# Summing two norms' squares over the partitions on GpSimd instead of TensorE

## The chip, the cores and the metric

The kernel runs on one core of one Trainium2 chip. The metric is the device time of one execution in microseconds; the median of a few runs stands for a kernel. A profiled execution gives, besides its own time, a trace of every instruction on every engine: TensorE (PE, with its weight loads as PEld), VectorE (DVE), ScalarE (ACT), GpSimd (POOL) and SyncE (SP), the last one only issuing transfers.

## The reference, cut to what matters

One layer of a streaming encoder is computed for a prompt of 256 frames and for 64 new frames of a running stream; the kernel treats them together as T = 320 columns. The model width D is 2048.

```python
def rmsnorm(x, g):
    x32 = x.astype(jnp.float32)
    y = x32 * lax.rsqrt(jnp.mean(x32 * x32, axis=-1, keepdims=True) + EPS)
    return (y * g.astype(jnp.float32)).astype(x.dtype)
...
    xn = rmsnorm(x, norm_mix[l])
    proj = xn @ w_in[l]
    q, k, v, u, vs, g = jnp.split(proj, [...], axis=-1)
    a = stick_breaking_prompt(q, k, v)          # or _sample, with the cache
    u = jax.nn.gelu(u)
    vs = rmsnorm(jax.nn.gelu(vs), sgu_norm[l])
    bb = spatial_gate(u, vs, w_spatial[l], b_spatial[l])
    gates = jax.nn.sigmoid(g + b_gate[l])
    merged = g_a * (a @ w_branch_a[l]) + g_b * (bb @ w_branch_b[l])
    h = x + merged @ w_out[l]
    hn = rmsnorm(h, norm_ffn[l])
    gu = hn @ w_gate_up[l]
    h = h + (jax.nn.silu(gu[..., :D_FF]) * gu[..., D_FF:]) @ w_down[l]
    return h, k, v, vs
```

After the layer a final RMSNorm follows. So there are four norms: of x (the first), of gelu(vs) over 1024 channels (the second), of h over 2048 (the third), and the final one.

## The kernel before, in words

Features lie on the 128 partitions, the 320 frames on the free axis. A norm needs, for each frame, the sum of squares over all features: first over the 128-feature tiles (elementwise adds into one 128x320 tile), then over the 128 partitions.

**Blocks.** All large products go through `block` (line 90): 128 output features, the sum over 16 (or 8, or 12) tiles of the input. Each weight tile is loaded by SP (line 80), 8 tiles of 128x128 at a time, into `raw`; ScalarE rounds it into `wh` (line 69) and VectorE writes the remainder `wl` (line 70). `product` (line 83) then issues three TensorE products for each tile: wh with the high part of the input (line 86), wh with the low part (line 87), wl with the high part (line 88). Eight tiles, so 24 products, are a half block here. `wh` and `wl` have four buffers each, `raw` three, and three more in the first part of the kernel. Block results go to three PSUM buffers `acc`, side results to `aux`.

**Ticks.** After each half block `tick()` (line 61) counts one up and issues what was put down for that tick with `at(...)`. This is how the side work is woven into the blocks by hand: attention (lines 293 to 381) at given ticks, and the second norm and the spatial gate as follows. `base` is the tick at which the last block of vs has been issued; at `base + 1` comes `sgu_norm` (line 444), at `base + 3 + 4p` `sgu_turn(p)` (scale vs by the norm and by its gain, store the new rows, transpose by DMA through SP), at `base + 5 + 4p` `sgu_join(p)` (VectorE puts the transposed halves together as `rows`), at `base + 6 + 4p` `sgu_mix(p)` (TensorE multiplies `rows` with the spatial weights, lines 464 and 465). The blocks of u run meanwhile. A scheduler turns the program into one queue for each engine and may move instructions of ScalarE and VectorE ahead of others in it.

**Norms.** `Squares.add` (line 152) squares a tile on ScalarE (lines 154, 157) and adds it to the total on GpSimd (line 158). `rms` (line 136) sums the total over the partitions: a product of a 128x128 tile of ones with the total, into the PSUM buffer `aux1` (line 138). That puts the sum on every partition. Then VectorE forms the mean plus EPS (line 140), ScalarE the square root (line 143), and `newton` (line 130) the reciprocal and a correction step on VectorE (lines 131 to 134). The first norm's sum is needed in the very first blocks (line 217, `rx`), the second by `sgu_turn` (line 450, `rv`), the third (line 533, `rh`) one tick into the first block of the FFN. The third norm is applied not before the FFN's products but after them, in `finish` (lines 542 and 545). The final norm has code of its own at the end and doesn't use `rms`.

**GpSimd** otherwise issues transfers: cache rows (lines 248, 251), k, v and sv stores (lines 400, 452), the residual x (line 526). It also sets the masks at the start. The kernel warms TensorE with products of ones at its start (line 167) and keeps it busy in the tail with some more (line 633).

Of the kernel before, what the change touches and what calls it, by code (L numbers as in the profile page):

```python
# [7 lines left out]

# [3 lines left out]
AF = mybir.ActivationFunctionType  # L12
ALU = mybir.AluOpType

P = 128
TP = 256
TS = 64
T = TP + TS
D = 2048
# [7 lines left out]
EPS = 1e-6  # L27
# [6 lines left out]
def stream_step(ctx: ExitStack, tc: tile.TileContext, xT, w_in, w_a, w_b, w_out, w_gu, w_down,  # L34
                gains, ws_t, bs, ck_t, cv, y_t, k_t, v_t, sv_t):
    nc = tc.nc
    pool = lambda name, bufs=1, **kw: ctx.enter_context(tc.tile_pool(name=name, bufs=bufs, **kw))
# [13 lines left out]
    def aux1():  # L51
        return psum.tile([P, 512], F32, tag="aux1", bufs=1, name="aux1")
# [13 lines left out]
    def halved(raw, n):  # L66
        wh = wsplit.tile([P, HALF * P], F32R, tag="wh", name="wh")
        wl = wsplit.tile([P, HALF * P], F32R, tag="wl", name="wl")
        nc.scalar.copy(out=wh[:, : n * P], in_=raw[:, : n * P])  # L69
        nc.vector.tensor_tensor(out=wl[:, : n * P], in0=raw[:, : n * P],  # L70
                                in1=wh[:, : n * P].bitcast(F32), op=ALU.subtract)
        return wh, wl
# [10 lines left out]
    def product(ps, w, j, x, first, last):  # L83
        wh, wl = w
        a, b = wh[:, j * P : (j + 1) * P], wl[:, j * P : (j + 1) * P]
        nc.tensor.matmul(ps[:, :T], a, x[0], start=first, stop=False)  # L86
        nc.tensor.matmul(ps[:, :T], a, x[1], start=False, stop=False)  # L87
        nc.tensor.matmul(ps[:, :T], b, x[0], start=False, stop=last)  # L88

    def block(src, act):  # L90
        ps = acc()
        nk = len(act)
        for k0 in range(0, nk, HALF):
            n = min(HALF, nk - k0)
            w = weights(src[:, k0 * P : (k0 + n) * P], n)
            for j in range(n):
                product(ps, w, j, act[k0 + j], k0 + j == 0, k0 + j == nk - 1)
            tick()
        return ps[:, :T]
# [4 lines left out]
    def pair(name, shape=(2, T), dt=F32):  # L104
        return big.tile([P, *shape], dt, tag="D", bufs=24, name=name)

    def gained(src, gain):
        hi, lo = slot("A"), slot("A")
        nc.scalar.activation(out=hi, in_=src, func=AF.Copy, scale=gain)  # L109
        nc.vector.scalar_tensor_tensor(out=lo, in0=src, scalar=gain, in1=hi.bitcast(F32),  # L110
                                       op0=ALU.mult, op1=ALU.subtract)
        return hi, lo

    def t320(tag, bufs=2, dt=F32):
        return tmp.tile([P, T], dt, tag=tag, bufs=bufs, name=tag)

    ones = const.tile([P, P], F32, name="ones")
# [5 lines left out]
    eps_t = const.tile([P, 1], F32, name="eps_t")  # L123
# [6 lines left out]
    def newton(r, ms, e):  # L130
        nc.vector.reciprocal(out=r, in_=r)
        nc.vector.scalar_tensor_tensor(out=e, in0=ms, scalar=-0.5, in1=r, op0=ALU.mult, op1=ALU.mult)
        nc.vector.tensor_tensor(out=e, in0=e, in1=r, op=ALU.mult)
        nc.vector.scalar_tensor_tensor(out=r, in0=e, scalar=1.5, in1=r, op0=ALU.add, op1=ALU.mult)

    def rms(name, total, width):
        ps = aux1()
        nc.tensor.matmul(ps[:, :T], ones, total, start=True, stop=True)
        ms = t320("ev")
        nc.vector.tensor_scalar(out=ms, in0=ps[:, :T], scalar1=1.0 / width, scalar2=EPS,  # L140
                                op0=ALU.mult, op1=ALU.add)
        r = const.tile([P, T], F32, tag="rms", bufs=2, name=name)
        nc.scalar.activation(out=r, in_=ps[:, :T], func=AF.Sqrt, bias=eps_t, scale=1.0 / width)
        newton(r, ms, t320("bb"))
        return r

# [14 lines left out]
    got = {}  # L161
    attn: dict[int, dict] = {0: {}}
    first = [[acc(), aux(), aux()], [acc(), aux(), aux()]]
    totx = const.tile([P, T], F32, tag="total", bufs=2, name="totx")
# [8 lines left out]
    def load_x(i, a=0, b=2):  # L173
        if i not in xp:
            xp[i] = pair("x")
        nc.sync.dma_start(out=xp[i][:, a:b, :], in_=xT[:, 2 * i + a : 2 * i + b, :])

    def load_w(b0, nb, c, n):
        raw = rpool.tile([P, HALF * P], F32, tag="raw1", bufs=9, name="raw1")
        nc.sync.dma_start(out=raw[:, : nb * n * P].rearrange("p (b k) -> p b k", b=nb),  # L180
                          in_=w_in[b0 : b0 + nb, :, c * P : (c + n) * P].rearrange("b p k -> p b k"))
        return raw

    def square(i):
        if i == 0:
            squares.append(pair("sqx"))
            nc.scalar.activation(out=squares[0], in_=xp[0], func=AF.Square)
        else:
            t = pair("xx")
            nc.scalar.activation(out=t, in_=xp[i], func=AF.Square)  # L190
            nc.vector.tensor_tensor(out=squares[0], in0=squares[0], in1=t, op=ALU.add)
# [6 lines left out]
    with tc.manual_schedule(engines={mybir.EngineType.SP}):  # L198
        load_x(0, 0, 1)
        for i, (b0, nb, c, n) in enumerate(tiles):  # L200
            raw = load_w(b0, nb, c, n)
            for more in behind.get(i, ()):
                load_x(*more)
            if i == len(tiles) - 1:
                for name, src in (("ck", ck_t[:, 0 : 2 * PAST]), ("cv", cv[:, :, 0 : 2 * P])):
                    attn[0][name] = t = pair(name, (2, PAST))
                    nc.sync.dma_start(out=t if name == "cv" else t.rearrange("p h t -> p (h t)"), in_=src)
            if i == 0:
                xs.append(gained(xp[0][:, 0, :], g_mix[:, 0:1]))
                lead = halved(raw, n)  # L210
                continue
            w = halved(raw, nb * n)
            for m in range(len(xs), c + n):
                xs.append(gained(xp[m // 2][:, m % 2, :], g_mix[:, m : m + 1]))
            if c + n == KD and b0 == 0:
                nc.vector.tensor_tensor(out=totx, in0=squares[0][:, 0, :], in1=squares[0][:, 1, :], op=ALU.add)
                got["rx"] = rms("rx", totx, D)
            if i == 1:
                for j in range(n):
                    for h, a in enumerate((lead, w)):  # L220
                        product(first[h][0], a, j, xs[j], j == 0, False)
                continue
            for b in range(nb):
                for j in range(n):
                    product(first[(b0 + b) % H][(b0 + b) // H], w, n * b + j, xs[c + j], c + j == 0, c + j == KD - 1)
            for m in done_squares.get(i, ()):
                square(m)
# [205 lines left out]
    for g in range(H):  # L433
        ps = block(w_in[4 * H + g], xs)
# [9 lines left out]
    def sgu_norm():  # L444
        got["rv"] = rms("rv", sq.total, H * P)
# [41 lines left out]
    for g in range(H):  # L487
        ps = block(w_in[3 * H + g], xs)
# [6 lines left out]
    for m in range(KD):  # L495
        gate = []
        for i in range(2):
            ps = block(w_in[5 * H + i * KD + m], xs)
# [9 lines left out]
        ps = block(w_a[m], aT)  # L508
        t = t320("mg", 1)
        nc.vector.tensor_tensor(out=t, in0=ps, in1=gate[0], op=ALU.mult)  # L510
        ps = block(w_b[m], bT)
# [10 lines left out]
    for m in range(KD):  # L522
# [4 lines left out]
        ps = block(w_out[m], merged)  # L527
# [3 lines left out]
        sq.add(hs[m])  # L531
    mctx.close()
    at(state["tick"] + 1, lambda: got.update(rh=rms("rh", sq.total, D)))

    sqf = Squares("sq_f")
# [68 lines left out]
    for s0, n in SLICES:  # L604
# [7 lines left out]
        for m in range(KD - LATE if final else KD):  # L612
            ps = block(w_down[m][:, s0 * P : (s0 + n) * P], halves)
# [24 lines left out]
    def root(ps, w):  # L638
        r, e = (const.tile([P, w], F32, name=f"{x}{w}") for x in "re")
        nc.scalar.activation(out=r, in_=ps[:, 0:w], func=AF.Abs_reciprocal_sqrt, scale=1.0 / D)  # L640
        nc.vector.scalar_tensor_tensor(out=e, in0=ps[:, 0:w], scalar=-0.5 / D, in1=r, op0=ALU.mult, op1=ALU.mult)
        nc.vector.tensor_tensor(out=e, in0=e, in1=r, op=ALU.mult)
        nc.vector.scalar_tensor_tensor(out=r, in0=e, scalar=1.5, in1=r, op0=ALU.add, op1=ALU.mult)
        return r
# [15 lines left out]
    with tc.manual_schedule(engines={mybir.EngineType.PE, mybir.EngineType.DVE, mybir.EngineType.Activation,  # L660
# [10 lines left out]
        r = root(sums, 2)  # L671
# [26 lines left out]
        r = root(sums, 1)  # L698
# [60 lines left out]
```

## Time and profile before

| | |
|---|---|
| median of 3 runs | 1705.58 us (1705.47 to 1706.55) |
| the profiled execution | 1705.79 us |
| its span, first to last instruction | 1704.0 us |
| granted TensorE clock, mean | 0.999 |
| TensorE busy | 1694.5 us, 11560 instructions |
| VectorE busy | 879.7 us, 1110 instructions |
| ScalarE busy | 673.8 us, 838 instructions |
| GpSimd busy | 54.9 us, 89 instructions |

How to read the lines that follow: in a timeline, a line gives the start and the length in microseconds, the engine, the line of the program, the operation, output tile<-input tiles, the shape, and how many instructions are merged in it; in brackets stands how long the engine had been idle before and what ended that. In a list of groups, the numbers behind the bar are the busy time in us, the mean length of one in ns, and the idle time before them. In a list for one line of the program, three lengths in ns are the shortest, the median and the longest. A line of the windows gives, for a stretch of time, the busy time of each engine with its number of instructions, the granted TensorE clock, the share of the DMA engines and GB/s.

### The profile page before, as it was taken

The numbers are of one execution on the slowest core, as the hardware profiler recorded it, in microseconds if no ns is written. First come the engines' busy times: TensorE is split into PE (matmuls) and PEld (weight loads), VectorE is DVE, ScalarE is ACT, GpSimd is POOL, SyncE is SP. The second block draws the span as 40 slices with busy tenths as digits, with TensorE's granted clock in tenths as the row PEclk, the third lists the DMA queues.
The fourth block names the chain that finished last, engine by engine and source line by source line (L and its number), as shares of the span: only waits on it lengthen the run. The fifth ranks groups of instructions, "written<-read, shape, count | busy, mean of one in ns | idle before, by whom it ended". The sixth has DMA issues, their size and how long they took to land.

```text
span 1704.0 us, 27430 instructions
## 1 busy us (share of the span) xinstructions
PE 1694.5 (99%) x11560; PEld 1690.2 (99%) x11560; DVE 879.7 (52%) x1110; ACT 673.8 (40%) x838; POOL 54.9 (3%) x89
## 2 busy tenths in 40 slices
PE   9999999999999999999999999999999999999998
PEld 9999999999999999999999999999999999999998
DVE  7665657544444445555444444444444444444456
ACT  6555655433333333444333332233333323333333
POOL 0200011000000001220000000000000000000000
PEclk9999999999999999999999999999999999999999
DMA  8766555444444445554444444444444444444454
GB/s 291 246 172 172 168 162 163 116 151 151 150 150 149 148 149 165 173 167 149 149 153 150 151 149 149 148 149 150 153 149 152 152 149 149 149 148 150 135 149 124
DMA packets 100411, 268.30 MB, mean 157 GB/s; under 512 B 29088, under 2 KB 35232, under 8 KB 100288
## 3 DMA queue, kind: packets, MB, share of 16 engines
q1 hardware_dynamic: 97520, 258.25, 48.4%
q0 software_dynamic: 2624, 8.26, 1.5%
q8 instruction: 90, 1.47, 0.3%
q14 instruction: 33, 0.27, 0.0%
q10 hardware_dynamic: 144, 0.05, 0.0%
HBM read 256.03 MB, written 5.51 MB: 153 GB/s over the span
## 4 chain that ended last, share of the span: by engine, by line
PE 99%; DVE 0%; DMA 0%; SPq 0%; ACT 0%; issue 0%; DVEq 0%
PE acc L86 32%; PE acc L87 32%; PE acc L88 31%; PE aux L88 1%; PE aux L87 1%; PE aux L86 1%; PE acc L573 0%; PE acc L589 0%; DVE h L651 0%; DMA x<-xT 0%; PE aux L464 0%; PE aux L367 0%; PE aux L573 0%; PE aux L307 0%; PE aux L294 0%; PE aux L296 0%
## 5 line engine op out<-in xcount | busy, mean ns | idle before, releaser
L69 ACT CAST wh<-raw 128x1024 fp32r<-128x1024 f32 (+1 forms) x476 | 491.3, 1032 | 964.9 <-PE acc L87 775.6
L70 DVE TENSOR_TENSOR wl<-raw,wh 128x1024 fp32r<-128x1024 f32 (+1 forms) x476 | 571.6, 1202 | 466.2 <-ACT wh L69 465.8
L86 PE MATMUL acc<-A,wh 128*128 128x320 f32 x2496 | 773.4, 310 | 0.7 <-ACT A L109 0.7
L87 PE MATMUL acc<-A,wh 128*128 128x320 f32 x2496 | 771.7, 309 | 0.0
L88 PE MATMUL acc<-A,wl 128*128 128x320 f32 x2496 | 771.4, 309 | 0.0
L86 PEld LDWEIGHTS acc<-A,wh 128*128 128x128 f32 x2496 | 468.8, 188 | 2.9 <-issue 1.5
L87 PEld LDWEIGHTS acc<-A,wh 128*128 128x128 f32 x2496 | 468.9, 188 | 0.5 <-DVE A L110 0.3
L88 PEld LDWEIGHTS acc<-A,wl 128*128 128x128 f32 x2496 | 468.8, 188 | 0.0
L86 PE MATMUL acc<-act,wh 128*128 128x320 f32 x656 | 202.7, 309 | 0.0
L87 PE MATMUL acc<-act,wh 128*128 128x320 f32 x656 | 202.7, 309 | 0.0
L88 PE MATMUL acc<-act,wl 128*128 128x320 f32 x656 | 202.7, 309 | 0.0
L86 PEld LDWEIGHTS acc<-act,wh 128*128 128x128 f32 x656 | 123.2, 188 | 0.0
L87 PEld LDWEIGHTS acc<-act,wh 128*128 128x128 f32 x656 | 123.2, 188 | 0.0
L88 PEld LDWEIGHTS acc<-act,wl 128*128 128x128 f32 x656 | 123.2, 188 | 0.0
L86 PE MATMUL acc<-mh,wh 128*128 128x320 f32 x256 | 79.1, 309 | 0.0
L87 PE MATMUL acc<-ml,wh 128*128 128x320 f32 x256 | 79.1, 309 | 0.0
L88 PE MATMUL acc<-mh,wl 128*128 128x320 f32 x256 | 79.1, 309 | 0.0
L545 DVE TENSOR_TENSOR bb<-acc,rh 128x320 f32<-128x320 f32 x44 | 21.6, 492 | 57.5 <-PE acc L88 57.5
L542 DVE TENSOR_TENSOR ev<-acc,rh 128x320 f32<-128x320 f32 x44 | 21.6, 492 | 56.6 <-PE acc L88 56.6
L86 PEld LDWEIGHTS acc<-mh,wh 128*128 128x128 f32 x256 | 48.0, 188 | 0.0
L87 PEld LDWEIGHTS acc<-ml,wh 128*128 128x128 f32 x256 | 48.0, 188 | 0.0
L88 PEld LDWEIGHTS acc<-mh,wl 128*128 128x128 f32 x256 | 48.0, 188 | 0.0
(205 smaller groups left out, 1153.3 us busy)
## 6 DMA issues: line engine op xcount, KB each, us to landing
raw<-w_gu SPq DMA_DIRECT2D x176, 512.0 KB, 3.6
raw<-w_in SPq DMA_DIRECT2D x141, 512.0 KB, 3.7
raw<-w_down SPq DMA_DIRECT2D x80, 512.0 KB, 3.5
raw<-w_out SPq DMA_DIRECT2D x32, 512.0 KB, 3.6
raw<-w_a SPq DMA_DIRECT2D x16, 512.0 KB, 3.5
raw<-w_b SPq DMA_DIRECT2D x16, 512.0 KB, 3.5
raw<-w_down SPq DMA_DIRECT2D x16, 256.0 KB, 2.7
xr<-xT POOLq DMA_DIRECT2D x16, 160.0 KB, 2.5
```

The lines of the kernel that those rows point to most:

```text
L69: nc.scalar.copy(out=wh[:, : n * P], in_=raw[:, : n * P])
L70: nc.vector.tensor_tensor(out=wl[:, : n * P], in0=raw[:, : n * P], in1=wh[:, : n * P].bitcast(F32), op=ALU.subtract)
L86: nc.tensor.matmul(ps[:, :T], a, x[0], start=first, stop=False)
L87: nc.tensor.matmul(ps[:, :T], a, x[1], start=False, stop=False)
L88: nc.tensor.matmul(ps[:, :T], b, x[0], start=False, stop=last)
L542: nc.vector.tensor_tensor(out=t, in0=pg, in1=got["rh"], op=ALU.mult)
L545: nc.vector.tensor_tensor(out=u, in0=pu, in1=got["rh"], op=ALU.mult)
```

## The change

In `rms`, the sum over the partitions is made by one GpSimd instruction that reads the total from SBUF and writes the sum to all 128 partitions of a new SBUF tile, `whole` (one buffer). The first norm keeps the product of ones: it passes False. What follows the sum is as before, reading `whole` in place of the PSUM tile.

```diff
-    def rms(name, total, width):
-        ps = aux1()
-        nc.tensor.matmul(ps[:, :T], ones, total, start=True, stop=True)
+    def rms(name, total, width, pool=True):
+        if pool:
+            whole = t320("whole", 1)
+            nc.gpsimd.partition_all_reduce(whole, total, P, ReduceOp.add)
+        else:
+            whole = aux1()[:, :T]
+            nc.tensor.matmul(whole, ones, total, start=True, stop=True)
         ms = t320("ev")
-        nc.vector.tensor_scalar(out=ms, in0=ps[:, :T], scalar1=1.0 / width, scalar2=EPS,
+        nc.vector.tensor_scalar(out=ms, in0=whole, scalar1=1.0 / width, scalar2=EPS,
                                 op0=ALU.mult, op1=ALU.add)
         r = const.tile([P, T], F32, tag="rms", bufs=2, name=name)
-        nc.scalar.activation(out=r, in_=ps[:, :T], func=AF.Sqrt, bias=eps_t, scale=1.0 / width)
+        nc.scalar.activation(out=r, in_=whole, func=AF.Sqrt, bias=eps_t, scale=1.0 / width)
         newton(r, ms, t320("bb"))
         return r
...
-                got["rx"] = rms("rx", totx, D)
+                got["rx"] = rms("rx", totx, D, False)
```

More of the change, by code (lines that the diff above doesn't have):

```diff
@@ L5 @@
 from concourse import mybir
+from concourse.bass_isa import ReduceOp
 from concourse.masks import make_identity
```

## The prediction

> **What bounds the kernel now.** I read the page first, then the timeline around the two places that change.
>
> ```profile
> span 1704.0 us, 27430 instructions
> PE 1694.5 (99%) x11560; PEld 1690.2 (99%) x11560; DVE 879.7 (52%) x1110; ACT 673.8 (40%) x838; POOL 54.9 (3%) x89
> PE 99%; DVE 0%; DMA 0%; SPq 0%; ACT 0%; issue 0%; DVEq 0%
> L70 DVE TENSOR_TENSOR wl<-raw,wh 128x1024 fp32r<-128x1024 f32 (+1 forms) x476 | 571.6, 1202 | 466.2 <-ACT wh L69 465.8
> raw<-w_in SPq DMA_DIRECT2D x141, 512.0 KB, 3.7
> ```
>
> TensorE is busy for 99% of the span, and 99% of the chain that ended last is TensorE. So a microsecond taken out of its queue is a microsecond won, and a microsecond in which its queue stands still is lost for good: nothing later can catch it up. VectorE, ScalarE and GpSimd matter only where TensorE, which works its queue in order, comes to a product whose operand isn't there. The question is how much sooner, and how much later, TensorE's operands come.
>
> **What is removed.** Two products of ones, each one pass through line 138. The timeline of TensorE at the third norm:
>
> ```profile
> 765.93 0.31 PE L88 MATMUL acc<-A,wl 128*128 128x320 f32 x1
> 766.07 0.70 PE L138 MATMUL aux<-sq_h,ones 128*128 128x320 f32 x2
> 766.37 0.55 PE L86 MATMUL acc<-A,wh 128*128 128x320 f32 x1
> 766.76 0.31 PE L87 MATMUL acc<-A,wh 128*128 128x320 f32 x1
> 766.90 0.31 PE L88 MATMUL acc<-A,wl 128*128 128x320 f32 x1
> ```
>
> Products follow each other every 0.14 to 0.15 us (766.76 to 766.90). From the L88 at 765.93 the L87 two places on would start at 766.22; it starts at 766.76. The product of ones therefore costs 0.54 us of the queue. Two of them: 1.1 us. That is 0.065% of the span, and all that this change can win. About 0.2%, or 3.4 us, is what a measurement here can tell from no change.
>
> **What is added, second norm.** GpSimd now adds over the partitions itself. Let Y be the time from the end of its last elementwise add of squares until the sums stand in SBUF, the fetching of whatever code the new instruction needs included. How long may Y be before TensorE waits? First what happens today, on GpSimd, ScalarE, VectorE and TensorE's weight loads in turn:
>
> ```profile
> 252.51 0.98 POOL L158 TENSOR_TENSOR sq_v<-sq_v,sq 128x320 f32<-128x320 f32 x1 [6.06 <-ACT sq L157]
> ...
> 255.03 1.28 ACT L143 ACT_TABLE_LOAD   x1
> 256.32 0.53 ACT L143 ACTIVATE rv<-aux,eps_t 128x320 f32<-128x320 f32 x1
> 258.02 1.05 ACT L69 CAST wh<-raw 128x1024 fp32r<-128x1024 f32 x1 [1.17 <-PE acc L87]
> ...
> 254.65 0.49 DVE L140 TENSOR_SCALAR ev<-aux 128x320 f32<-128x320 f32 x1 [1.90 <-PE aux L138]
> 255.06 1.22 DVE L70 TENSOR_TENSOR wl<-raw,wh 128x1024 fp32r<-128x1024 f32 x1
> 256.88 2.15 DVE L131 RECIPROCAL rv<-rv 128x320 f32<-128x320 f32 x1 [0.61 <-ACT rv L143]
> 261.35 0.49 DVE L134 SCALAR_TENSOR_TENSOR rv<-bb,rv 128x320 f32<-128x320 f32 x1
> 269.89 0.96 DVE L284 COPY rows<-turned 128x640 uint16<-128x640 uint16 x2 [1.55 <-DMA sv_t<-vs]
> ...
> 271.90 1.00 PEld L464 LDWEIGHTS aux<-wst,rows 128*128 128x128 f32 x8
> ```
>
> The last add ends at 253.49. The root starts at 256.32; behind it lie the reciprocal and Newton step, the scaling of vs, the transpose by DMA and the copy into rows, which ends at 270.85: 14.53 us from root to rows. The mixing products of line 464 read rows, and TensorE gets to them at 271.90, only 1.05 us later. With the product of ones gone it gets there at 271.35. So the sums have to be there by 271.35 - 14.53 = 256.82, or Y = 3.3 us. Beyond that TensorE stands before line 464 for Y - 3.3, if the mixing products keep their place in its queue.
>
> The new waits are on ScalarE's root and VectorE's line 140, since both read the sums. Queued behind them are the next casts (258.02) and subtractions (255.06) that make TensorE's weights; behind the transpose on SP's queue are the loads of raw, each 3.7 us to landing. These have four buffers of lead, which the third norm measures. GpSimd's own queue behind the sum holds the stores of sv_t, which need the norm anyway.
>
> **What is added, third norm.** Here nothing in TensorE's queue reads the result soon; only the weights can run out.
>
> ```profile
> 764.56 1.09 POOL L158 TENSOR_TENSOR sq_h<-sq_h,sq 128x320 f32<-128x320 f32 x1 [5.95 <-ACT sq L157]
> ...
> 766.81 0.49 DVE L140 TENSOR_SCALAR ev<-aux 128x320 f32<-128x320 f32 x1 [0.81 <-PE aux L138]
> 767.22 1.22 DVE L70 TENSOR_TENSOR wl<-raw,wh 128x1024 fp32r<-128x1024 f32 x1
> 777.37 0.49 DVE L545 TENSOR_TENSOR bb<-acc,rh 128x320 f32<-128x320 f32 x1 [1.31 <-PE acc L88]
> ```
>
> The subtraction at 767.22 fills the buffer that TensorE needs four half blocks later, when it has finished the second block, which line 545 marks (777.2; 776.7 without the product of ones). Line 140 ahead of it and the subtraction itself take 0.41 and 1.22, so the sums must be there by 775.05. The last add ends at 765.65: Y may be 9.4 us. Beyond that TensorE loses Y - 9.4. Reordering the two would hardly help, since VectorE is also held up while GpSimd reads:
>
> ```profile
> L110 DVE SCALAR_TENSOR_TENSOR A<-x,gain,A x16: 543/546/554, 4.0 to 33.7; 128x320 fp32r<-128x320 f32 x16
> L110 DVE SCALAR_TENSOR_TENSOR A<-h,gain,A x16: 545/1168/1170, 659.3 to 764.8; 128x320 fp32r<-128x320 f32 x16
> ```
>
> The same instruction takes 0.546 us while GpSimd is idle and 1.168 beside its add of squares.
>
> **What Y is.** No row shows the new instruction. GpSimd's nearest rows:
>
> ```profile
> L158 POOL TENSOR_TENSOR sq_h<-sq_h,sq 128x320 f32<-128x320 f32 x15 | 16.2, 1081 | 18.1 <-ACT sq L157 18.1
> L231 POOL COPY xr<-rx 128x1 f32<-128x1 f32 x2 | 0.8, 425 | 0.0
> L124 POOL MEMSET eps_t<- 128x1 f32 x1 | 0.1, 98 | 0.0
> ```
>
> From below, one pass over the same tile: 1.08 us. From above, 128 partitions one after another, each at what the smallest copy costs, 0.425 us: 54.4 us. I take the first row as the nearer, because it reads and writes the same 128x320 tile: 128 partitions fold in seven halvings, 7 x 1.08 = 7.6 us. For code that must first be fetched I add what one load takes from issue to landing, 3.7 us; its own bounds are nothing and twice that. Y = 11.3 us, an estimate. Whatever GpSimd has to fetch back before it next adds squares (third norm) has hundreds of microseconds of its idle time to hide in.
>
> **What a stall costs beyond itself.** The windows at the end of the kernel, where TensorE's work ends at 1697.0 (the column ahead of the DMA share is its granted clock), and the same products of ones at the start and at the end:
>
> ```profile
> 1696.00:1697.00 1.00, 1.00 (x8) 0.71 (x6) 0.91 (x5) 0.00 (x0) 0.00 (x0) 1.00 0.79 247
> ...
> 1699.00:1700.00 1.00, 0.00 (x0) 0.00 (x0) 0.90 (x4) 0.00 (x0) 0.00 (x0) 0.64 0.94 261
> 1700.00:1701.00 1.00, 0.00 (x0) 0.00 (x0) 0.00 (x0) 0.00 (x0) 0.00 (x0) 0.50 0.91 252
> ...
> 1.00 3.78 PE L167 MATMUL aux<-ones 128*128 128x128 f32 x16 [1.00 <-POOL eps_t L124]
> 1695.47 1.14 PE L633 MATMUL aux<-ones 128*128 128x128 f32 x8
> ```
>
> A mean of 0.64 means that the clock halved 0.28 us into that window: 2.3 us after the last product. Getting it back: 16 pieces took 3.78 us from rest, 0.236 each, against 1.14 / 8 = 0.143 when warm, so 16 x 0.094 = 1.5 us. I add 1.5 for each stall of over 2.3 us.
>
> **The sum.** Second norm 11.3 - 3.3 = 8.0, third norm 11.3 - 9.4 = 1.9, one restart 1.5, less 1.1: +10.3 us. The profiled execution took 1705.79 us (its span of 1704.0 and 1.8 around it), 0.2 above the median of the runs, 1705.58. Against that median: 1715.9. With Y from 6.3 to 17 us this case runs from 3.0 + 0 + 1.5 - 1.1 = +3.4 to 13.7 + 7.6 + 3.0 - 1.1 = +23.2, that is 1709.0 to 1728.8.
>
> **Rivals.**
>
> *It is hidden (not slower).* One mechanism: the sums, code and all, are there within 6.3 us of the last add, or the mixing products are put further back in TensorE's queue by as much as the sums come late, so that Y - 3.3 isn't paid in full. It decides at line 464: a stall there of up to 3.0 us, with its restart and less 1.1, stays within 3.4. For it speaks that GpSimd's pass is short (1.08) and that casts and subtractions already stand out of program order, four half blocks ahead. Against it: every group of other products in TensorE's queue starts between half blocks, where the program puts it, as the product of line 138 above does, and 6.3 us leaves little for both folding and code. Time: 1704.5 (nothing stalls) to 1709.0, about 1706. Chance 0.29.
>
> *The sum goes partition by partition.* If the fold is serial, Y lies between the forecast and the upper bound: 128 steps at a middle price between 0.098 (the smallest memset, line 124 above) and 0.425 are 33 us. Then 29.7 + 23.6 + 3.0 - 1.1 = +55: 1761. It begins at Y over 17, +23 us.
>
> For it: nothing in the trace shows lanes of GpSimd exchanging data, so nothing shows halvings. Against: an instruction made for this should do better than 128 separate ones. Chance 0.24. The Trainium skill, GPSIMD Engine Reference, section 3.2, speaks against the change here: it reports 247,699 ns for a reduction over the partitions of 128x2048, which in proportion is an estimated 38.7 us for 320 columns; section 2.1 adds about 6 us for the first call to freshly loaded code. By these two figures Y would be 44.7 and the kernel 41.4 + 35.3 + 3.0 - 1.1 = 78.6 us slower. No row shows that instruction, and it need not be the same one; as one form of the serial case I give this price 0.06 of the 0.24.
>
> **The numbers.** The forecast has 0.45, the hidden case 0.29, the serial case 0.24. Nothing in the sum wins more than 1.1 us, so faster by over 0.2% has 0.02, for a new order elsewhere. Same: 0.29; slower: 0.45 + 0.24 = 0.69. The range starts at 1704.5, where all is hidden, and ends at 1750, in the middle of the serial case (Y about 28), leaving out some 0.15.
>
> **What would show it.** Right: line 138 only once on TensorE; TensorE idle before line 464 for about 8 us, released by VectorE's rows, with the granted clock under 1 just after; a small wait on subtractions around 777; VectorE's line 140 and ScalarE's root released by GpSimd about 11 us after the last add. Wrong: TensorE's idle time unchanged (hidden), the mixing products in the middle of a half block (reordered), stalls of tens of microseconds at both places (serial), or GpSimd's sum done within 3 us.

## The result, and the profile after

The changed kernel takes 1709.84 us (median of 13 runs, 1708.09 to 1710.81) against 1705.75 us before (13 runs beside them, 1705.25 to 1706.55): 4.1 us slower, ratio 1.0023 with an interval of [1.0015, 1.0031]. The forecast had the sign and the range right, but its +10.3 us is two and a half times what was measured. The profiled execution took 1709.80 us. In the experiments below, one execution of the run "third norm only" took 4872.45 us and is left out of its median.

The change puts five lines into the program, so that line 86 of before is line 87 now, 158 is 163, 464 is 469. The page:

```profile
span 1708.0 us, 27428 instructions
PE 1695.5 (99%) x11556; PEld 1690.2 (99%) x11556; DVE 878.1 (51%) x1110; ACT 673.5 (39%) x838; POOL 59.7 (3%) x91
PE 96%; issue 1%; DMA 1%; DVE 1%; POOL 0%; SPq 0%; ACT 0%; DVEq 0%; POOLq 0%; ACTq 0%
```

TensorE is still busy for 99%, but the chain that ended last now leaves it for 4% of the span. The groups on GpSimd show the new instruction and what stands ahead of it (the numbers behind the second bar are idle time before it and its releaser):

```profile
L140 POOL PARTITION_ALL_REDUCE whole<-sq_h x1 | 2.2, 2231 | 6.1 <-issue 6.1
L140 POOL PARTITION_ALL_REDUCE whole<-sq_v x1 | 2.2, 2167 | 6.6 <-issue 6.6
```

The fold of 128x320 takes 2.2 us. Ahead of it GpSimd stands idle for 6.1 and 6.6 us, "issue": it waits for no other engine. The trace has a pair of short instructions there, MODIFY_POOL_CONFIG, from the same line 140, which the views leave out: at 253.50 and 253.54 for the second norm, at 770.36 and 770.40 for the third. An experiment below shows that the idle time behind the pair is the fetching of the code. The second norm in the timeline, on GpSimd, ScalarE and VectorE in turn:

```profile
252.34 0.98 POOL L163 TENSOR_TENSOR sq_v<-sq_v,sq 128x320 f32<-128x320 f32 x1 [6.06 <-ACT sq L162]
259.87 2.17 POOL L140 PARTITION_ALL_REDUCE whole<-sq_v  x1 [6.55 <-issue]
...
262.07 0.57 ACT L148 ACTIVATE rv<-whole,eps_t 128x320 f32<-128x320 f32 x1 [2.41 <-POOL whole L140]
...
258.39 1.22 DVE L71 TENSOR_TENSOR wl<-raw,wh 128x1024 fp32r<-128x1024 f32 x1 [2.29 <-ACT wh L70]
262.07 0.33 DVE L145 TENSOR_SCALAR ev<-whole 128x320 f32<-128x320 f32 x1 [2.45 <-POOL whole L140]
276.32 0.93 DVE L289 COPY rows<-turned 128x640 uint16<-128x640 uint16 x2 [1.55 <-DMA sv_t<-vs]
```

The last add ends at 253.32, the sums stand at 262.04: the prediction's Y is 8.7 us. The subtraction of 258.39 has gone ahead of line 145, which before stood in front of one. The rows end at 277.25. Now TensorE, first the mixing group before the change and then after it:

```profile
272.05 1.05 PE L464 MATMUL aux<-wst,rows 128*128 128x128 f32 x8
```

```profile
274.72 0.31 PE L89 MATMUL acc<-A,wl 128*128 128x320 f32 x1
277.40 2.05 PE L469 MATMUL aux<-wst,rows 128*128 128x128 f32 x8 [2.37 <-DVE rows L289]
279.24 0.63 PE L470 MATMUL aux<-wd,rows 128*128 128x128 f32 x2
...
292.56 1.13 PE L469 MATMUL aux<-wst,rows 128*128 128x128 f32 x8 [0.95 <-DVE rows L289]
```

and two windows of it:

```profile
275.00:280.00 5.00, 2.63 (x13) 2.63 (x13) 1.88 (x5) 1.00 (x1) 0.54 (x1) 0.70 0.73 254
280.00:285.00 5.00, 5.00 (x35) 5.00 (x35) 3.58 (x7) 2.11 (x4) 0.00 (x0) 0.96 0.31 105
```

Before the first mixing group TensorE stands still for 2.5 us (277.40 is 2.68 behind the product ahead of it, and 0.15 is usual). Before the second group (292.56) it stands still once more, idle for 0.95, which with the 0.16 us by which a product's row outlasts its place in the queue makes 1.1 us. The same eight pieces of line 464 took 1.05 us before and take 2.05 now, at a granted clock of 0.70 and 0.96: at half clock for 0.30 x 5 / 0.5 = 3.0 us in the first window and 0.4 in the second, some 3 us of it with products running. That loses about 1.5 us. (A granted clock of 0.50 is the lowest that any window here shows, so a mean of 0.70 is read as 0.30 / 0.5 of the window at half.)

The mixing groups have also moved in TensorE's queue. Ahead of the first one stand 1704 products of lines 87 to 89, where before there were 1680: it stands 24 products, a half block, later. Ahead of the second there are 1782 in place of 1776: it stands six products into a half block. Its rows pass through ScalarE, which splits the first group's result (L481) before it copies the second's input (L276):

```profile
282.34 0.73 ACT L481 CAST bh<-mix 128x640 fp32r<-128x640 f32 x1 [6.33 <-DVE mix L479]
...
284.95 0.60 ACT L276 COPY flat<-vs 128x512 uint16<-128x512 uint16 x1
```

The third norm, GpSimd and then VectorE:

```profile
769.09 1.09 POOL L163 TENSOR_TENSOR sq_h<-sq_h,sq 128x320 f32<-128x320 f32 x1 [5.95 <-ACT sq L162]
776.28 2.23 POOL L140 PARTITION_ALL_REDUCE whole<-sq_h  x1 [6.11 <-issue]
...
775.25 1.23 DVE L71 TENSOR_TENSOR wl<-raw,wh 128x1024 fp32r<-128x1024 f32 x1 [2.29 <-ACT wh L70]
778.54 0.33 DVE L145 TENSOR_SCALAR ev<-whole 128x320 f32<-128x320 f32 x1 [2.06 <-POOL whole L140]
```

Y is 8.3 us here, and TensorE doesn't wait: its whole list of waits holds no entry of note but the two before line 469.

```profile
PE aux L469 <- DVE rows L289: 3.3, 2, 2.4
PE aux L172 <- POOL eps_t L125: 1.0, 1, 1.0
...
PE acc L89 <- DVE wl L71: 0.2, 1, 0.2
```

The two last adds of squares split the loss. From 252.51 to 764.56 it was 512.05 us before, from 252.34 to 769.09 it is 516.75: +4.70. From there to the end of the span it was 939.44 and is 938.91: -0.53, the product of ones that is gone. And 2.5 + 1.1 + 1.5 - 0.54 = 4.6 of the 4.70.

### The profile page after: what moved, and what is told of

Its sections match the earlier page's. It is cut to its first block, busy times and chain, and to the rows that moved or that the text cites. A ratio compares the mean times of both kernels' runs of the same rounds, so it can differ in the third digit from the quotient of the medians.

```text
span 1708.0 us, 27428 instructions
## 1 busy us (share of the span) xinstructions
PE 1695.5 (99%) x11556; PEld 1690.2 (99%) x11556; DVE 878.1 (51%) x1110; ACT 673.5 (39%) x838; POOL 59.7 (3%) x91
## 3 DMA queue, kind: packets, MB, share of 16 engines
q0 software_dynamic: 2624, 8.26, 1.6%
## 4 chain that ended last, share of the span: by engine, by line
PE 96%; issue 1%; DMA 1%; DVE 1%; POOL 0%; SPq 0%; ACT 0%; DVEq 0%; POOLq 0%; ACTq 0%
PE acc L87 31%; PE acc L89 31%; PE acc L88 31%; PE acc L578 0%; PE aux L87 0%; PE aux L89 0%; PE aux L88 0%; PE acc L594 0%; DMA raw<-w_in 0%; PE aux L469 0%; DMA turned<-flat 0%; DVE h L656 0%; PE aux L372 0%; DMA sv_t<-vs 0%; PE aux L578 0%
```

## The experiments

The theory, "late rows": the sums of the second norm come late (code and fold), so rows come late for the mixing products, and TensorE's waits there with the clock restart are the whole loss. The rival: the new instruction costs wherever it stands, because it holds VectorE while it reads and blocks VectorE's and ScalarE's queues. All times are medians; "before" is the kernel before on the same chip in the same session; there were three sessions, each on another chip. An interval reaches some 1.5 us to either side, so a row within 1.5 us of 0 can't be told from no change by its time alone.

| run | median us | before us | difference | ratio [interval] |
|---|---|---|---|---|
| third norm only | 1705.22 | 1705.91 | -0.7 | 0.9996 [0.9987, 1.0004] |
| second norm only | 1710.04 | 1705.91 | +4.1 | 1.0022 [1.0013, 1.0032] |
| later mixing | 1705.42 | 1705.91 | -0.5 | 0.9997 [0.9988, 1.0005] |
| later mixing, ones | 1706.21 | 1705.91 | +0.3 | 1.0001 [0.9992, 1.0009] |
| code early | 1705.60 | 1705.96 | -0.4 | 0.9999 [0.9990, 1.0007] |
| place kept | 1713.60 | 1705.96 | +7.6 | 1.0045 [1.0032, 1.0058] |
| half later | 1709.17 | 1705.96 | +3.2 | 1.0018 [1.0010, 1.0027] |
| half later, 12 ones | 1708.78 | 1705.96 | +2.8 | 1.0018 [1.0009, 1.0027] |
| half later, 6 ones | 1707.37 | 1705.85 | +1.5 | 1.0008 [1.0000, 1.0017] |
| code early, half later | 1704.83 | 1705.85 | -1.0 | 0.9994 [0.9985, 1.0003] |

**Which norm.** Two runs that each do one half of the change:

```diff
-        got["rv"] = rms("rv", sq.total, H * P)
+        got["rv"] = rms("rv", sq.total, H * P, False)
```

> The second norm goes back to the product of ones; only the third is summed on GpSimd. Theory (late rows: the code load and the fold make rows late for line 469 after the second norm, and TensorE's wait there with its clock restart is the whole loss): the third norm costs nothing and wins 0.54 us, so about 1705.2, 0.5 us under the kernel before, no wait of TensorE around 777. Rival (the instruction itself costs, by holding VectorE while it reads or by blocking its and ScalarE's queues): a good part of the 4.1 us stays, +1 to +3 us over the kernel before.

```diff
-    at(state["tick"] + 1, lambda: got.update(rh=rms("rh", sq.total, D)))
+    at(state["tick"] + 1, lambda: got.update(rh=rms("rh", sq.total, D, False)))
```

> Only the second norm is summed on GpSimd; the third goes back to the product of ones. Late rows: all of the loss and 0.54 us more, +4.6 us over the kernel before. Rival (the instruction itself costs wherever it stands): about half of the loss, +2 us.

The third norm alone: -0.7 us, as late rows had it. GpSimd's code load and fold are there as in the changed kernel (5.97 and 2.36 us) and cost nothing:

```profile
771.57 2.36 POOL L140 PARTITION_ALL_REDUCE whole<-sq_h  x1 [5.97 <-issue]
```

The second alone: +4.1 us, as much as the whole change and within half a microsecond of the expected 4.6, with both waits in TensorE's timeline:

```profile
278.11 1.27 PE L469 MATMUL aux<-wst,rows 128*128 128x128 f32 x8 [2.25 <-DVE rows L289]
...
293.45 1.13 PE L469 MATMUL aux<-wst,rows 128*128 128x128 f32 x8 [1.00 <-DVE rows L289]
```

The rival's even shares didn't come.

**More time for the rows.**

```diff
-        at(base + 5 + 4 * p, sgu_join, p)
-        at(base + 6 + 4 * p, sgu_mix, p)
+        at(base + (7, 10, 13, 17)[p], sgu_join, p)
+        at(base + (8, 11, 14, 18)[p], sgu_mix, p)
```

> The changed kernel with the join and the mixing products at ticks 7, 10, 13, 17 and 8, 11, 14, 18 in place of 5, 9, 13, 17 and 6, 10, 14, 18: the rows have 3.5 to 7 us more until TensorE comes to them. Late rows: no wait before line 469, no restart of the clock, both products of ones won: 1.1 us under the kernel before, about 1704.7. Rival (the instruction itself costs): still 2 to 4 us over the kernel before, as in the changed kernel.

The same edit in the kernel before:

> The control of the run with later mixing: the kernel before, products of ones for all three norms, with the same later ticks. Late rows: nothing waits there before, so nothing to win, 0 within 0.4 us of the kernel before. If the later ticks are themselves a gain, 1 us or more under it, and the run with later mixing on GpSimd would owe that much to them.

With GpSimd's sums as late as ever, the loss is gone: -0.5. The control gained nothing (+0.3), so the later ticks are no gain in themselves. Of the 1.1 us expected half is missing: this timeline still has one short wait, since the transposed rows took longer to arrive.

```profile
279.75 1.13 PE L469 MATMUL aux<-wst,rows 128*128 128x128 f32 x8 [0.62 <-DVE rows L289]
```

**The code.**

```diff
-        sq.add(v)
+        sq.add(v, nc.vector if g == H - 1 else None)
+        if g == H - 2:
+            early = const.tile([P, 1], F32, name="early")
+            tc.keep_in_program_order(nc.gpsimd.partition_all_reduce(early, v[:, 0:1], P, ReduceOp.add))
```

> The last add of squares of the second norm goes to VectorE, and before it GpSimd makes a sum over the partitions of one column that nobody reads, so that its code is there when the real sum comes. The mixing products are free to stand where the scheduler puts them. Late rows: the sums are there some 3 us after the last add, within the slack of 3.3 us; no wait before line 469, no restart, about 1 us under the kernel before (1704.8); the idle time of 6.5 us before the real sum is gone. Rival (the fold or its reading is what costs, not the code): still +2 to +4 us.

```profile
252.55 0.68 POOL L447 PARTITION_ALL_REDUCE early<-vs  x1 [6.30 <-issue]
253.14 2.25 POOL L140 PARTITION_ALL_REDUCE whole<-sq_v  x1
...
272.52 1.13 PE L472 MATMUL aux<-wst,rows 128*128 128x128 f32 x8 [1.04 <-DVE rows L289]
```

The 6.3 us now stand before the one-column sum, which itself takes 0.68, and the real one follows with nothing between. The pair MODIFY_POOL_CONFIG stands on line 447 now, at 246.44 and 246.48, and none is left on line 140 for this norm. So the wait belongs to the first use of this instruction after elementwise adds, not to its size: it is the code. The loss of 4.1 us becomes -0.4. The edit also moves the last add to VectorE, where it ends at 252.96 instead of 253.32; that 0.36 us is small beside the 6.6 us of waiting. A wait of 1.0 is left where none was expected: the sums are there at 255.4, in time by the prediction's 256.82, but rows end at 272.37, 17 us after the root began at 255.42 instead of the 14.5 us before, with VectorE idle for 2.96 us before the copy into rows, waiting for a transfer.

**The place in the queue.** The first product behind each mixing group is pinned behind it:

```diff
-        nc.tensor.matmul(ps[:, :T], a, x[0], start=first, stop=False)
+        c = nc.tensor.matmul(ps[:, :T], a, x[0], start=first, stop=False)
+        if state.pop("pin", False):
+            tc.keep_in_program_order(c)
...
+        state["pin"] = True
         b, u = pair("mix"), us[p]
```

> The changed kernel with the first product after each mixing group pinned behind it, so that the mixing products keep the place that the program gives them; in the changed kernel the first group stands one half block later. Late rows: rows are ready about 277.2 as there, TensorE gets to line 469 at about 271.2, so it waits 6.0 us in place of 2.6, with one clock restart of 1.5 and less 1.1: +6.4 us over the kernel before. If the place in the queue plays no part, +4.1 as in the changed kernel.

```profile
277.75 2.05 PE L471 MATMUL aux<-wst,rows 128*128 128x128 f32 x8 [6.35 <-DVE rows L291]
```

```profile
275.00:280.00 5.00, 2.25 (x11) 2.29 (x11) 1.53 (x4) 0.00 (x0) 0.54 (x1) 0.63 0.77 252
280.00:285.00 5.00, 5.00 (x27) 5.00 (x26) 2.44 (x5) 2.53 (x6) 0.00 (x0) 0.68 0.02 3
```

The wait is 6.35 + 0.16 = 6.5 us, against 6.0 expected, and the kernel 7.6 us slower, against 6.4. The rest is the clock: at 0.68 in the second window it is at half for 0.32 x 5 / 0.5 = 3.2 us more, to 283.2, so from 277.75 on for 5.4 us; that loses 2.7, not 1.5. (In the first window it is at half for 0.37 x 5 / 0.5 = 3.7 us, from 276.3 on, the last 2.2 of them with products.) Then 6.5 + 2.7 - 1.1 = 8.1, beside 1711.8 - 1704.0 = 7.8 us between the spans.

**The clock.** The first mixing group where the scheduler had put it, the second later, so that only the first wait is left:

```diff
-        at(base + 5 + 4 * p, sgu_join, p)
-        at(base + 6 + 4 * p, sgu_mix, p)
+        at(base + (5, 10, 13, 17)[p], sgu_join, p)
+        at(base + (7, 11, 14, 18)[p], sgu_mix, p)
```

> The changed kernel with mixing at ticks 7, 11, 14, 18 and the second and third join one tick later: the first group stands where the scheduler has put it anyway, the second a half block later than the program had it. Late rows: the first wait of 2.6 us and its restart stay, the second wait of 0.95 is gone: 2.6 + 1.5 - 1.1 = +3.0 us over the kernel before.

and the same with products of ones in that wait, twelve and then six:

```diff
         vn = turns.pop(p)
+        if p == 0:
+            idle = aux1()
+            for _ in range(12):
+                tc.keep_in_program_order(nc.tensor.matmul(idle[:, :P], ones, ones, start=True, stop=True))
```

> The run with the half later mixing, plus twelve products of ones (0.143 us each, 1.7 us) on TensorE just ahead of the first mixing group, in the time in which it waits. If the clock restart is part of the loss: the wait left is 0.9 us, the granted clock stays 1.00 there, and the kernel is 1.5 us faster than the run without the products of ones, +1.5 us over the kernel before. If the clock plays no part, the same time as without them, +3.0 or what that run shows.

> The run with the half later mixing, plus six products of ones (0.237 us each, 1.4 us) in the 2.3 us in which TensorE waits for the first rows; twelve took 2.8 us, more than the wait. If the clock restart is part of the loss: a wait of 0.9 us is left, the granted clock stays 1.00, and the mixing stretch is 1.5 us shorter than without them; over all executions the median falls by most of that, to about 1707.7, and the granted clocks of the runs no longer spread from 0.996 to 0.999. If the clock plays no part: 1709.2, as without them.

TensorE's timeline without products of ones, with twelve, and with six:

```profile
278.09 1.13 PE L469 MATMUL aux<-wst,rows 128*128 128x128 f32 x8 [2.34 <-DVE rows L289]
...
294.89 1.05 PE L469 MATMUL aux<-wst,rows 128*128 128x128 f32 x8
```

```profile
275.05 2.84 PE L468 MATMUL aux<-ones 128*128 128x128 f32 x24
277.82 1.13 PE L473 MATMUL aux<-wst,rows 128*128 128x128 f32 x8
...
293.09 1.05 PE L473 MATMUL aux<-wst,rows 128*128 128x128 f32 x8
```

```profile
274.92 1.50 PE L468 MATMUL aux<-ones 128*128 128x128 f32 x12
277.80 1.13 PE L473 MATMUL aux<-wst,rows 128*128 128x128 f32 x8 [1.38 <-DVE rows L289]
...
293.07 1.05 PE L473 MATMUL aux<-wst,rows 128*128 128x128 f32 x8
```

The two windows from 275 us on, without products of ones:

```profile
275.00:280.00 5.00, 2.66 (x19) 2.42 (x18) 2.71 (x7) 1.04 (x1) 0.85 (x2) 0.93 0.96 266
280.00:285.00 5.00, 5.00 (x27) 5.00 (x27) 2.55 (x6) 1.31 (x2) 0.00 (x0) 0.73 0.34 120
```

and with six:

```profile
275.00:280.00 5.00, 3.62 (x30) 3.46 (x29) 3.28 (x7) 1.04 (x1) 0.54 (x1) 1.00 0.90 263
280.00:285.00 5.00, 5.00 (x36) 5.00 (x35) 3.10 (x5) 3.49 (x7) 0.00 (x0) 1.00 0.44 132
```

From the first to the second mixing group the same work takes 16.80 us without them (294.89 - 278.09) and 15.27 with twelve or with six. So keeping TensorE busy through part of the wait saves 1.5 us, and the granted clock, the number after the five engines, stays at 1.00 where it was 0.93 and 0.73. The loss against the kernel before falls from 3.2 us (half later) to 1.5 (six ones, on another chip). The two intervals overlap, so the saving rests on the timelines and on the clocks: the runs' mean granted clocks, 0.996 to 0.999 over eleven runs without, are 0.999 in all eleven with six. The runs without also show that the restart isn't paid in every execution: the three at 0.999 took 1706.78 to 1707.56 us, the eight below that 1708.1 to 1710.96.

The windows say when the clock changed, and it isn't at a fixed time after the last product. In the changed kernel it went to half at 277.0, 2.1 us after it. Half later it did so at 280 - 0.07 x 5 / 0.5 = 279.3, 3.7 us after it, when products had been running again for 1.2 us. With the place kept it did so at 276.3, 5.1 us after it. It stayed there for 3.4 us, 3.4 us and, by windows of 0.5 us, 6.8 us.

Twelve were a misjudged size: I had counted 0.143 us for each, but a product of ones is two pieces, 0.237 together, so they filled the whole wait. Their median fell by only 0.4, and the traced execution has another 1.2 us in its last store, which no run here explains.

**Both cures at once**, the early code and the half later mixing:

> Both cures: the code is fetched early (last add of squares on VectorE, a one-column sum on GpSimd before it) and the mixing products come half a block later (ticks 7, 11, 14, 18). Late rows: no wait at any mixing group, so both products of ones are won whole, 1.1 us under the kernel before (1704.8), at the mixing stretch as at the third norm 0.54 each. If something else of the new instruction still costs, 0 or more over the kernel before.

```profile
252.12 0.66 POOL L447 PARTITION_ALL_REDUCE early<-vs  x1 [6.31 <-issue]
252.69 2.25 POOL L140 PARTITION_ALL_REDUCE whole<-sq_v  x1
...
274.39 1.05 PE L472 MATMUL aux<-wst,rows 128*128 128x128 f32 x8
...
289.59 1.05 PE L472 MATMUL aux<-wst,rows 128*128 128x128 f32 x8
```

No wait at either group, and 1704.83 us (1704.22 to 1705.17) against 1705.85 (1705.12 to 1706.55): the 1.0 us that two products of ones are worth. The ranges of the runs hardly touch, but the interval of the ratio, [0.9985, 1.0003], still holds 1: by that measure it is the fastest kernel of the study and not proven faster than the one before.

## Why the prediction was right and wrong, point by point

- *What is removed*: right, 1.1 us. The stretch after the third norm is 0.53 shorter, and with both waits cured the kernel wins 1.0.
- *Y*: mis-sized. 11.3 us were forecast, 8.7 and 8.3 measured. The split was wrong too: the fold is 2.2 us, as long as two passes of 1.08 and not seven (7.6), and the code is 6.1 to 6.6 and not 3.7. It is luck that these two errors, of opposite sign, half cancel in Y.
- *Third norm*: Y as measured is below the bound of 9.4 us, so the forecast loss of 1.9 became nothing. The new order, with a subtraction ahead of line 145, gave more room still.
- *Second norm*: the mechanism was right (rows late, TensorE waits before line 469), its size was not. With the measured Y the prediction's own rule gives 8.7 - 3.3 = 5.4 us; 2.5 were paid. The step that failed is "if the mixing products keep their place in its queue". The first group stands one half block later: 24 products of 0.146 are 3.5 us, and 272.05 + 3.5 - 0.54 - 0.17 (the changed kernel is that much ahead at its last add) + 2.5 is the 277.4 of the timeline. With the place kept the wait is 6.5 us and the kernel 7.6 slower; there the rows also came 15.6 us after the root (262.02 to 277.60) and not 14.5. The move is the second half of the rival "hidden", and the measured 1709.84 lies just above the 1709.0 at which that rival ends. My argument against it, that every group starts between half blocks, doesn't hold: the first group does so a half block later, and the second stands inside one.
- *The second group's wait*, 1.1 us, was not in the sum at all: its rows come through the same ScalarE queue, behind the first group's results, as the two ScalarE lines of the result show.
- *A stall's restart*: right in kind, and right at 1.5 us for the short wait. The long one cost 2.7, because the clock stayed at half for twice as long, which the prediction's fixed price didn't have. Nor is there a fixed 2.3 us after which the clock falls, and in some executions of "half later" nothing was paid.
- *The serial case* is refuted: the fold is 2.2 us. The Trainium skill's figure for a reduction over the partitions (GPSIMD Engine Reference, section 3.2), an estimated 38.7 us in proportion, isn't this instruction's. Its 6 us for a first call to freshly loaded code (section 2.1) agrees with the 6.0 to 6.7 us measured here.

With what was measured the sum is 2.5 + 1.1 + 1.5 - 1.1 = +4.0 us. Of the 6.3 us between this and the forecast, the size of Y makes 2.6 at the second norm and 1.9 at the third, and the move in the queue makes 2.9 (5.4 - 2.5); the second group's wait, left out of the sum, takes 1.1 of it back.

## What to carry to other kernels

Moving work off the bottleneck engine wins its own time there at most, here 1.1 us, and what replaces it is judged by its latency up to the next operand that the bottleneck waits for: look for the consumer with the least slack, here 1.05 us. An instruction that uses other code than its engine's usual ones costs the fetch each time the engine switches; put a first, tiny use of it where nobody waits. A schedule may shift the waiting products by itself, so a forecast should price the wait for both places.

## What the runs showed of the hardware

- GpSimd's sum over the partitions took 2.17 to 2.36 us for 128x320 and 0.66 to 0.68 us for 128x1; the idle time ahead of its first use after elementwise adds was 5.97 to 6.74 us in every run that has it.
- Going back costs too. In the changed kernel GpSimd stands still for 7.9 us before its first mask instruction and for 7.7 before the first add of the third norm, where the kernel before had nothing or 0.45 us. The pair MODIFY_POOL_CONFIG stands ahead of both. Before the mask it is there in the kernel before as well, but the instruction follows it within 0.1 us: it costs only when other code ran last. The two half runs agree. With the third norm alone the wait is 8.26 us before the mask and 0.46 before the add; with the second alone it is 0.29 before the mask and 7.76 before the add. So what GpSimd used last seems to stay loaded into the next execution. Both waits are hidden, since "code early, half later" has them and loses nothing.

```profile
665.99 1.09 POOL L163 TENSOR_TENSOR sq_h<-sq_h,sq 128x320 f32<-128x320 f32 x1 [0.46 <-ACT sq L162]
```

```profile
678.66 0.89 POOL L163 TENSOR_TENSOR sq_h<-sq_h,sq 128x320 f32<-128x320 f32 x1 [7.76 <-ACT A L110]
```

- TensorE's granted clock went to half where TensorE had been idle for 2.25 to 6.35 us. That came 2.1 to 5.1 us after the last product and lasted 3.4 us, or 6.8 with the longest wait. Idle times of 0.95 to 1.38 us left it at 1.00.
